# Hybrid decoder block: attention's constants, R products, t2 sums and the last tokens rearranged

## The chip, the cores and the metric

The kernel runs on one core of one Trainium2 chip. The metric is the device time of one execution in microseconds (us). A program written with a tile framework is planned ahead: the framework takes the instructions in the order of the source, gives each engine a fixed order of its own by a simulated schedule, and adds the semaphores. On the chip every engine then runs its own list strictly in that order.

The engines are TensorE (PE, with PEld for its weight loads), VectorE (DVE), the scalar engine (ACT), GpSimd (POOL) and SyncE (SP). SP issues the plain loads and stores, POOL the loads that add to what is already in the tile.

## The reference

One decoder layer on 512 tokens of width 1024, all float32:

```python
h = rmsnorm(x, pre_mix_norm)
q_r, k_r, v_r, g_r, q_s, k_s, v_s, gate_r, gate_s = split(h @ w_in)
ret = swish(g_r) * groupnorm(retention_chunkwise(q_r, k_r, v_r))    # 4 heads of 128/256
swa = swa_gqa_sinks(q_s, k_s, v_s, sinks)      # 8 heads of 64, window 128, 2 key heads
merged = sigmoid(gate_r) * (ret @ w_ret_out) + sigmoid(gate_s) * (swa @ w_swa_out)
x = x + rmsnorm(merged @ w_out, post_mix_norm)
u = square(relu(rmsnorm(x, pre_mlp_norm) @ w_up))                   # 4096 wide
out = x + rmsnorm(u @ w_down, post_mlp_norm)
```

## The kernel before, in words

**Splits.** Every operand of a product is written as a rounded high part and a low remainder: `split` casts on ACT (L123) and subtracts on VectorE (L124). `mm3` makes three matmuls of it: high by high (L166), high by low (L167), low by high (L168). `parts` gives each split weight a `whi` and a `wlo` from a ring of four buffers; raw weights come through a ring of two.

**The start.** Key and value weights and x transposed (`xTs`) are loaded in turn, then two value weights, then x by tokens (`xts`), all by SP in this order. The first projections are made from x times the gain (`xg`), before the token norms are known, and scaled afterwards. `token_factors` squares each token's row on ACT and raises it to the power -0.5 on POOL; a matmul with ones spreads the four factors over the partitions in `R_ps`, which ACT copies to `R` (L348). `norm_input(k)` multiplies `xTs[k]` by `R` (L351; odd k on POOL, even k on VectorE) and splits the result into `hT`, from which every later projection is made. These calls stand in the source after the first key projection, ordered behind the last instructions of the first queries (`qs_last`) and of the doubled keys (`kk_last`), each on its engine.

The pool `xpool` of the first stage is closed, and `rpool`, `dpool` and `asmall` of attention are opened where it lay. `dpool` begins with the constants: `dist_sb` (distances and mask), `decay_sb`, `chunk_sb` and `sink_sb`, each with its load on SP (L396 to L402).

**Attention, head 0.** `swa_queries` projects the queries (`pblk`), multiplies by `R` into `rg` (L386) and splits into `qs2` (L416, L417). POOL doubles the keys into `kk2` (L614), TensorE transposes them, and a split gives `ksT`. `swa_scores` first forms `bias` from `dist_sb` on VectorE (L433), then makes 16 score matmuls (L444). The last value block (`v0_block(3)`) stands before them on TensorE, the projection of the retention queries behind them.

**The last stage.** The product of `u` (`uc`) with `w_down` is made by a Winograd scheme of seven products, p1 to p7, over four chunks j of the inner dimension, in two token blocks `tb` of 128 for each half. Chunk j of the weights lies in `tch[j]` (128x2048) and becomes, in place, one sum of weight blocks after another: `t_add` issues a POOL load that adds a block. `step_p5(j)` uses `tch[j]`; the sum for `step_p6(j)` is then added by such a load for j below `T2_DMA` = 2, and on VectorE from `rb[j]` (L1092) for j = 2 and 3. `left` splits an activation block from a ring of two, `right` splits a weight chunk in two halves.

**The end.** `combine(tb)` puts products together and calls `finish` for tokens `tb` and `2 + tb`. `finish(t, n, src)` squares a column half on ACT (L1059), multiplies it by the gain `g_out` in place (L1064, L1071) and, when both halves are there, raises the mean to -0.5 on POOL (`rf`, L1070), adds the residual `x1` (L1074) and stores. The last product p4 runs j = 0 and 1 with a `combine` behind each, then j = 2 and 3 for each token block in turn:

```python
    for tb in range(2):
        for j in (2, 3):
            for h in range(2):
                product(p4, *ab[j - 2], h, False, j == 3, tb)
        nc.vector.tensor_tensor(u3[tb], p4[tb], u3[tb], op=ALU.subtract)
        finish(2 + tb, 0, u3[tb])
```

Of the kernel before, what the change touches and what calls it, by code (L numbers as in the profile page):

```python
# [16 lines left out]
P = 128  # L17
# [20 lines left out]
POOL_K = (1, 3, 5, 7)  # L38
QS_AT = 1
LEFT_AHEAD = 300  # L40
T2_DMA = 2
# [52 lines left out]
def block_kernel(ctx, tc, x, xT, pre_mix, w_in, w_gate, w_ret, w_swa, w_out, sinks, post_mix,  # L94
# [25 lines left out]

    def split(hi, lo, src):

        nc.scalar.copy(hi, src)  # L123
        nc.vector.tensor_tensor(lo, src, f(hi), op=ALU.subtract)  # L124
# [223 lines left out]
    nc.scalar.copy(R, R_ps)  # L348

    def norm_input(k):  # L350
        (nc.gpsimd if k in POOL_K else nc.vector).tensor_tensor(xTs[k], xTs[k], R, op=ALU.mult)  # L351
        split_scaled(hT[0][:, k], hT[1][:, k], xTs[k], gT[:, k : k + 1])
# [41 lines left out]

    dist_sb = dpool.tile([P, 2 * P], F32, name="dist_sb", bufs=1)
    nc.sync.dma_start(dist_sb, dist)  # L396
    decay_sb = dpool.tile([P, RET_HEADS, P], F32, name="decay_sb", bufs=1)
    nc.sync.dma_start(decay_sb, decay)
    chunk_sb = dpool.tile([P, 2, RET_HEADS], F32, name="chunk_sb", bufs=1)
    nc.sync.dma_start(chunk_sb, chunk)  # L400
    sink_sb = dpool.tile([P, SWA_HEADS], F32, name="sink_sb", bufs=1)
# [3 lines left out]
    def swa_queries(w, first=False):  # L405

        if first:
            ps = rpool.tile([P, SEQ], F32, name="rg", bufs=2)
            project_copy(ps, w, True)
        else:  # L410
            ps = project_block(w)
        rows = [slice(g * SWA_DH, (g + 1) * SWA_DH) for g in range(2)]
        qs2 = []
        for g in range(2):
            q2 = dpool.tile([P, SEQ], F32R, name=f"qs2{g}", bufs=1)
            last_hi = nc.scalar.mul(q2[rows[g]], ps[rows[g]], SWA_DH**-0.5)  # L416
            last = nc.vector.scalar_tensor_tensor(  # L417
                q2[rows[1 - g]], ps[rows[g]], SWA_DH**-0.5, f(q2[rows[g]]),
                op0=ALU.mult, op1=ALU.subtract,
            )  # L420
            qs2.append(q2)
        return (qs2, (last_hi, last)) if first else qs2
# [189 lines left out]
    for g in range(SWA_KV):  # L612
        for i in range(2):
            kk_last = nc.gpsimd.tensor_copy(kk2[:, g, :, i, :], kv[:, :, g * SWA_DH : (g + 1) * SWA_DH])  # L614
        ps = bank([P, SEQ])
        for t in range(NT):
            nc.tensor.transpose(
                ps[:, t * P : (t + 1) * P], kk2[:, g, t].rearrange("p i d -> p (i d)"), ident
            )
        split(ksT[0][:, g, :], ksT[1][:, g, :], ps)  # L620
    v0_block(3)
    v0_out(3)
    for h in range(RET_HEADS):
# [10 lines left out]
        if h == 0:  # L634
            with ExitStack() as order:
                for ins in (*qs_last, kk_last):
                    order.enter_context(tc.issue_after(ins.ins))
                for k in range(KD):
                    norm_input(k)
            uctx0.close()  # L640
            actx = ExitStack()
            apool = actx.enter_context(tc.tile_pool(name="apool", bufs=1, side="right"))
            retT = [apool.tile([P, KD, SEQ], F32R, name=f"retT{i}") for i in range(2)]
            swaT = [apool.tile([P, 4, SEQ], F32R, name=f"swaT{i}") for i in range(2)]
# [409 lines left out]
    def finish(t, n, src):  # L1054

        c = slice(n * 512, (n + 1) * 512)
        junk = junks.tile([P, 512], F32, name="junk2")
        ss = small.tile([P, 1], F32, name=f"ssf{n}")
        nc.scalar.activation(junk, src, AF.Square, accum_out=ss)  # L1059
        if outz[t] is None:  # L1060
            outz[t] = src
            ms0[t] = small.tile([P, 1], F32, name="ms0")
            nc.vector.tensor_scalar(ms0[t], ss, 1.0 / D_MODEL, EPS, op0=ALU.mult, op1=ALU.add)
            nc.vector.tensor_tensor(src, src, g_out[:, c], op=ALU.mult)  # L1064
            return
        r = small.tile([P, 1], F32, name="rf")
        nc.vector.tensor_scalar(
            ss, ss, 1.0 / D_MODEL, ms0[t][:, 0:1], op0=ALU.mult, op1=ALU.add
        )
        nc.gpsimd.tensor_tensor(r, ss, mhalf[:, 0:1], op=ALU.pow)  # L1070
        nc.vector.tensor_tensor(src, src, g_out[:, c], op=ALU.mult)  # L1071
        for i, z in ((1 - n, outz[t]), (n, src)):
            c = slice(i * 512, (i + 1) * 512)
# [3 lines left out]
            nc.sync.dma_start(out[t * P : (t + 1) * P, c], z)  # L1077


    for tb in range(2):  # L1080
# [3 lines left out]
        finish(tb, 0, v)  # L1084
# [35 lines left out]
    def combine(tb):  # L1120
# [3 lines left out]
        finish(tb, 1, p1c[tb])  # L1124
# [3 lines left out]
        finish(2 + tb, 1, v)  # L1128
# [43 lines left out]
```

## Time and profile before

| | |
|---|---|
| median of 3 runs | 754.84 us (754.82, 754.84, 758.47) |
| profiled execution, its own time | 760.68 us |
| its span, first to last instruction | 758.9 us |
| TensorE busy, matmuls | 742.0 us (98%), 4654 |
| VectorE busy | 546.3 us (72%) |
| scalar engine busy | 399.1 us (53%) |
| GpSimd busy | 55.3 us (7%) |
| mean granted TensorE clock | 0.991 |
| HBM read | 104.48 MB, 140 GB/s over the span |

Times in the profile are counted from the first instruction. A busy TensorE row counts a matmul from its start to its modelled end, and neighbours overlap; so its pace is read from the distance of the starts. The granted clock is 1.00 at 2.4 GHz and 0.50 at 1.2 GHz. A bracket at the end of a row says how long the engine was idle before the instruction and what ended that; "issue" there means that the profile shows nothing for which it waited. The end of a load is not in its row: it is the issue time plus the time to landing of the DMA view.

### The profile page before, as it was taken

The page shows a single profiled execution, that of the slowest core. Times are in us where ns is not written, and L with a number is a line of the kernel's source. Part 1 is how long each engine was busy: PE and PEld are TensorE (multiplying, and loading weights), DVE is VectorE, ACT ScalarE, POOL GpSimd, SP SyncE. Part 2 cuts the span into 40 slices and gives each one's busy share as a digit, 9 for nine tenths or more (in the row PEclk, how much of TensorE's full clock was granted, in tenths as well). Part 3 has the DMA queues.
Part 4 walks back from the last instruction along what each step waited for, and adds up shares of the span by engine and source line. Part 5 has one row for each costly group of instructions (what it writes and reads, how often), then busy time and mean ns, then how long its engine had stood idle before and what let it go on. Part 6 is the DMA issues. An engine that isn't in the chain of part 4 may idle for free.

```text
span 758.9 us, 11653 instructions
## 1 busy us (share of the span) xinstructions
PE 742.0 (98%) x4654; PEld 669.1 (88%) x4654; DVE 546.3 (72%) x840; ACT 399.1 (53%) x640; POOL 55.3 (7%) x69
## 2 busy tenths in 40 slices
PE   8989999999999999999999999999999999999986
PEld 8879889898888989899888999999999888888864
DVE  5386483664868867776754776678878788978795
ACT  6574453365554544343552764655656656555560
POOL 0500000000001000000001200000000010010010
PEclk9989999999999999999999999999999999999998
DMA  8613322312016585553482426866763998198511
GB/s 303 191 55 85 111 57 84 111 29 84 29 56 153 137 236 128 139 145 108 153 304 109 111 79 204 201 180 185 177 157 136 302 270 183 59 202 183 111 57 55
DMA packets 51430, 107.32 MB, mean 141 GB/s; under 512 B 3376, under 2 KB 31152, under 8 KB 47536
## 3 DMA queue, kind: packets, MB, share of 16 engines
q1 hardware_dynamic: 46336, 80.89, 32.1%
q0 software_dynamic: 5040, 25.69, 18.2%
q8 instruction: 36, 0.59, 0.3%
q14 instruction: 18, 0.15, 0.1%
HBM read 104.48 MB, written 2.10 MB: 140 GB/s over the span
## 4 chain that ended last, share of the span: by engine, by line
PE 77%; DVE 9%; DMA 8%; issue 4%; ACT 2%; SPq 0%; POOL 0%; POOLq 0%; DVEq 0%; ACTq 0%
PE p L167 5%; PE wino L168 5%; PE p L168 5%; PE p L166 5%; PE wino L166 5%; PE wino L167 5%; PE pblk L166 5%; PE pblk L167 5%; PE pblk L168 5%; DMA raw<-in_w_up 4%; DVE wlo L124 2%; PE ptok L168 2%; PE ptok L167 2%; PE ptok L166 2%; PE yr L168 2%
## 5 line engine op out<-in xcount | busy, mean ns | idle before, releaser
L124 DVE TENSOR_TENSOR wlo<-raw,whi 128x1024 fp32r<-128x1024 f32 x89 | 108.5, 1221 | 76.5 <-ACT whi L123 73.4
L123 ACT CAST whi<-raw 128x1024 fp32r<-128x1024 f32 x89 | 93.2, 1050 | 113.5 <-PE pblk L167 35.8
L167 PE MATMUL p<-wlo,left 128*128 128x512 f32 x224 | 88.2, 394 | 2.3 <-DVE wlo L124 2.2
L168 PE MATMUL p<-whi,left 128*128 128x512 f32 x224 | 87.7, 392 | 0.2 <-DVE left L124 0.2
L166 PE MATMUL p<-whi,left 128*128 128x512 f32 x224 | 87.5, 392 | 0.1
L166 PE MATMUL pblk<-hT,whi 128*128 128x512 f32 x136 | 53.2, 391 | 0.0
L167 PE MATMUL pblk<-hT,whi 128*128 128x512 f32 x136 | 53.0, 389 | 0.0
L168 PE MATMUL pblk<-hT,wlo 128*128 128x512 f32 x136 | 52.9, 389 | 0.0
L167 PEld LDWEIGHTS p<-wlo,left 128*128 128x128 f32 x224 | 42.4, 189 | 11.8 <-DVE wlo L124 3.1
L168 PEld LDWEIGHTS p<-whi,left 128*128 128x128 f32 x224 | 42.5, 190 | 9.4 <-DVE left L124 0.6
L166 PEld LDWEIGHTS p<-whi,left 128*128 128x128 f32 x224 | 42.3, 189 | 9.4 <-ACT left L123 0.5
L123 ACT CAST left<-uc 128x1024 fp32r<-128x1024 f32 x28 | 29.3, 1049 | 25.3 <-PE p L167 25.3
L124 DVE TENSOR_TENSOR left<-uc,left 128x1024 fp32r<-128x1024 f32 x28 | 34.1, 1221 | 10.5 <-ACT left L123 10.5
L124 DVE TENSOR_TENSOR wlo<-tch,whi 128x1024 fp32r<-128x1024 f32 x32 | 38.6, 1220 | 2.1 <-ACT whi L123 2.1
L123 ACT CAST whi<-tch 128x1024 fp32r<-128x1024 f32 x32 | 33.4, 1045 | 10.6 <-PE p L168 7.2
L123 ACT CAST whi<-rs 128x1024 fp32r<-128x1024 f32 x21 | 22.0, 1049 | 29.7 <-PE yr L167 11.1
L124 DVE TENSOR_TENSOR wlo<-rs,whi 128x1024 fp32r<-128x1024 f32 x21 | 25.6, 1218 | 9.4 <-ACT whi L123 9.4
L168 PE MATMUL wino<-h2s,p 128*128 128x256 f32 x104 | 29.8, 287 | 1.0 <-DVE p L124 1.0
L967 ACT ACTIVATE uc<-uc 128x512 f32<-128x512 f32 x26 | 15.0, 624 | 29.5 <-DVE uc L255 29.5
L168 PEld LDWEIGHTS pblk<-hT,wlo 128*128 128x128 f32 x136 | 25.5, 188 | 5.3
L166 PEld LDWEIGHTS pblk<-hT,whi 128*128 128x128 f32 x136 | 25.5, 188 | 5.0
L167 PEld LDWEIGHTS pblk<-hT,whi 128*128 128x128 f32 x136 | 25.5, 188 | 4.9
(321 smaller groups left out, 2330.6 us busy)
## 6 DMA issues: line engine op xcount, KB each, us to landing
tch<-in_w_down POOLq DMA_DIRECT2D x10, 1024.0 KB, 9.2
raw<-in_w_in SPq DMA_DIRECT2D x14, 512.0 KB, 5.4
raw<-in_w_in SPq DMA_DIRECT2D x7, 1024.0 KB, 5.5
raw<-in_w_down SPq DMA_DIRECT2D x7, 1024.0 KB, 7.6
rs<-in_w_up SPq DMA_DIRECT2D x13, 512.0 KB, 4.3
rs<-in_w_up POOLq DMA_DIRECT2D x13, 512.0 KB, 5.7
raw<-in_w_up SPq DMA_DIRECT2D x13, 512.0 KB, 5.1
raw<-in_w_gate SPq DMA_DIRECT2D x8, 512.0 KB, 4.5
```

The source lines that it names most:

```text
L123: nc.scalar.copy(hi, src)
L124: nc.vector.tensor_tensor(lo, src, f(hi), op=ALU.subtract)
L166: nc.tensor.matmul(ps, ah, bh, start=first, stop=False)
L167: nc.tensor.matmul(ps, ah, bl, start=False, stop=False)
L168: nc.tensor.matmul(ps, al, bh, start=False, stop=last)
L967: nc.scalar.activation(rb, rb, AF.Relu, scale=(1.0, -1.0)[b])
```

## The change

Five edits. (1) The four constants get a pool of their own, `cpool`, opened behind `dpool` and `asmall` instead of at the head of `dpool`. (2) `R`'s copy gets the priority that the token factors have, and all eight products of `xTs` with `R` go to VectorE, at the place of that copy; `norm_input` keeps only the splits, ordered behind `qs_last` alone. (3) `T2_DMA` becomes 4: the sum for `step_p6` comes by an adding load for all four chunks. (4) `finish` is taken apart into `squares`, `weigh`, `factor` and `residual`. The gains of the four token blocks that `combine` finishes stand behind the splits of chunks 2 and 3, and the residuals of the first two blocks are ordered behind the last split (`issue_after` orders the instructions of its block that run on the same engine as the one it names). (5) p4 for the last token block ends its first sum after j = 1; j = 2 and 3 are made for two halves of 256 columns, each in a bank of its own, with its own sum, square and gain product, the latter into a fresh tile.

```diff
-POOL_K = (1, 3, 5, 7)
-T2_DMA = 2
+T2_DMA = 4
...
     def split(hi, lo, src):
         nc.scalar.copy(hi, src)
-        nc.vector.tensor_tensor(lo, src, f(hi), op=ALU.subtract)
+        last["split"] = nc.vector.tensor_tensor(lo, src, f(hi), op=ALU.subtract)
...
-    nc.scalar.copy(R, R_ps)
+    with tc.high_priority(offset=FACTORS_AHEAD):
+        nc.scalar.copy(R, R_ps)
+    for k in range(KD):
+        nc.vector.tensor_tensor(xTs[k], xTs[k], R, op=ALU.mult)
     def norm_input(k):
-        (nc.gpsimd if k in POOL_K else nc.vector).tensor_tensor(xTs[k], xTs[k], R, op=ALU.mult)
         split_scaled(hT[0][:, k], hT[1][:, k], xTs[k], gT[:, k : k + 1])
...
-    dist_sb = dpool.tile([P, 2 * P], F32, name="dist_sb", bufs=1)
+    cpool = bctx.enter_context(tc.tile_pool(name="cpool", bufs=1))
+    dist_sb = cpool.tile([P, 2 * P], F32, name="dist_sb")
     nc.sync.dma_start(dist_sb, dist)
...
-                for ins in (*qs_last, kk_last):
+                for ins in qs_last:
                     order.enter_context(tc.issue_after(ins.ins))
...
-    def product(ps, a, b, h, first, last, tb):
+    def product(ps, a, b, h, first, last, tb, c=slice(0, 512)):
...
-                tuple(o[:, i % 2] for o in b[h]), first and i == 0, last and i == 3,
+                tuple(o[:, i % 2, c] for o in b[h]), first and i == 0, last and i == 3,
...
-    def finish(t, n, src):
...
+    def squares(t, i, src):
+        w = src.shape[1]
         junk = junks.tile([P, 512], F32, name="junk2")
+        ss = fin.tile([P, 1], F32, name="ssf", bufs=9)
+        nc.scalar.activation(junk[:, :w], src, AF.Square, accum_out=ss)
+        ms = fin.tile([P, 1], F32, name="msf", bufs=9)
+        rest = EPS if i == 0 else ms0[t][:, 0:1]
+        nc.vector.tensor_scalar(ms, ss, 1.0 / D_MODEL, rest, op0=ALU.mult, op1=ALU.add)
+        ms0[t] = ms
+    def residual(t, r, parts_of):
+        for c0, z in parts_of:
+            c = slice(c0, c0 + z.shape[1])
             nc.vector.scalar_tensor_tensor(
                 z, z, r[:, 0:1], x1[t][:, c], op0=ALU.mult, op1=ALU.add
             )
             nc.sync.dma_start(out[t * P : (t + 1) * P, c], z)
+    def factor(t):
+        r = fin.tile([P, 1], F32, name="rf", bufs=4)
+        nc.gpsimd.tensor_tensor(r, ms0[t], mhalf[:, 0:1], op=ALU.pow)
+        return r
+    def weigh(n, src):
+        nc.vector.tensor_tensor(src, src, g_out[:, n * 512 : (n + 1) * 512], op=ALU.mult)
...
     for j in range(2):
-        product2(p4, j, left(j, 3), right(tch[j]))
+        a, b = left(j, 3), right(tch[j])
+        for h in range(2):
+            for tb in range(2):
+                product(p4, a, b, h, j == 0, j == 1 and tb == 1, tb)
         combine(j)
     ab = [(left(j, 3), right(tch[j])) for j in (2, 3)]
     for tb in range(2):
+        weigh(1, outz[2 + tb])
+        weigh(1, p1c[tb])
+    with tc.issue_after(last["split"].ins):
+        for tb in range(2):
+            residual(tb, factor(tb), ((0, outz[tb]), (512, p1c[tb])))
+    for j in (2, 3):
+        for h in range(2):
+            product(p4, *ab[j - 2], h, False, j == 3, 0)
+    nc.vector.tensor_tensor(u3[0], p4[0], u3[0], op=ALU.subtract)
+    squares(2, 1, u3[0])
+    weigh(0, u3[0])
+    residual(2, factor(2), ((512, outz[2]), (0, u3[0])))
+    nc.vector.tensor_tensor(u3[1], p4[1], u3[1], op=ALU.subtract)
+    zs = []
+    for i in range(2):
+        c = slice(i * 256, (i + 1) * 256)
+        ps = bank([P, 256], "p4c")
         for j in (2, 3):
             for h in range(2):
-                product(p4, *ab[j - 2], h, False, j == 3, tb)
-        nc.vector.tensor_tensor(u3[tb], p4[tb], u3[tb], op=ALU.subtract)
-        finish(2 + tb, 0, u3[tb])
+                product([None, ps], *ab[j - 2], h, j == 2, j == 3, 1, c)
+        z = junks.tile([P, 512], F32, name="junk2")[:, :256]
+        nc.vector.tensor_tensor(u3[1][:, c], ps, u3[1][:, c], op=ALU.add)
+        squares(3, 1 + i, u3[1][:, c])
+        nc.vector.tensor_tensor(z, u3[1][:, c], g_out[:, c], op=ALU.mult)
+        zs.append((i * 256, z))
+    residual(3, factor(3), [(512, outz[3])] + zs)
```

## Rows read from the trace of the kernel before

**Rows 1.** Timeline of TensorE, 726 to 752: start, duration, line, tile, idle before.
```profile
726.48 0.39 PE L166 MATMUL p<-whi,left 128*128 128x512 f32 x1
...
736.70 0.39 PE L166 MATMUL p<-whi,left 128*128 128x512 f32 x1
739.25 0.79 PE L167 MATMUL p<-wlo,left 128*128 128x512 f32 x1 [2.16 <-DVE wlo L124]
...
751.33 0.39 PE L168 MATMUL p<-whi,left 128*128 128x512 f32 x1
```

**Rows 2.** Chain that ended last, 94 to 97: start, length.
```profile
94.49 1.92 PE swa_s L444 x16
```

**Rows 3.** Busy time by stretch; behind the engines granted clock, DMA share, GB/s.
```profile
12.00:16.00 4.00, 4.00 (x36) 4.00 (x36) 2.73 (x5) 2.65 (x5) 0.00 (x0) 1.00 1.06 365
...
36.70:46.30 9.60, 6.62 (x26) 5.57 (x25) 9.36 (x29) 8.95 (x22) 0.00 (x0) 0.64 0.35 110
736.70:742.70 6.00, 3.84 (x11) 2.73 (x10) 6.00 (x8) 3.15 (x5) 0.00 (x0) 0.72 0.10 37
642.00:660.00 18.00, 17.92 (x80) 14.49 (x78) 18.00 (x21) 11.63 (x16) 0.00 (x0) 1.00 0.24 73
...
666.00:672.00 6.00, 5.93 (x26) 4.76 (x26) 5.99 (x6) 2.81 (x4) 1.24 (x2) 1.00 1.05 208
```

**Rows 4.** Timeline of TensorE, 38 to 47.
```profile
39.15 0.63 PE L444 MATMUL swa_s<-ksT,qs 128*128 128x256 f32 x2 [2.16 <-DVE qs L417]
40.59 3.36 PE L444 MATMUL swa_s<-ksT,qs 128*128 128x256 f32 x14 [0.82 <-DVE ksT L124]
43.75 0.63 PE L166 MATMUL pblk<-xg,whi 128*128 128x512 f32 x1
...
46.27 0.40 PE L166 MATMUL pblk<-xg,whi 128*128 128x512 f32 x1
```

**Rows 5.** Timeline of VectorE, 28 to 42.
```profile
28.79 0.87 DVE L301 SCALAR_TENSOR_TENSOR v<-ptok,rstd,v 128x256 fp32r<-128x256 f32 x2
36.15 0.50 DVE L433 TENSOR_SCALAR bias<-dist_sb 128x256 f32<-128x256 f32 x2 [6.48 <-issue]
...
38.41 1.40 DVE L417 SCALAR_TENSOR_TENSOR qs<-rg,qs 64x512 fp32r<-64x512 f32 x2
39.84 1.29 DVE L124 TENSOR_TENSOR ksT<-ps,ksT 128x512 fp32r<-128x512 f32 x2
```

**Rows 6.** Timeline of SP's queue, 29 to 31.
```profile
29.46 0.44 SPq L396 DMA_DIRECT2D dist_sb<-in_dist  x1
```

**Rows 7.** DMA issues in 29.2 to 29.5: count, size, us to landing.
```profile
dist_sb<-in_dist SPq DMA_DIRECT2D x1, 128.0 KB, 6.6
```

**Rows 8.** Timeline of VectorE, 730 to 736.
```profile
734.25 0.76 DVE L1074 SCALAR_TENSOR_TENSOR c<-c,rf,x 128x512 f32<-128x512 f32 x1 [0.44 <-POOL rf L1070]
```

**Rows 9.** Timeline of VectorE and SP's queue behind the last matmul.
```profile
751.75 0.69 DVE L1138 TENSOR_TENSOR u<-p,u 128x512 f32<-128x512 f32 x1 [1.29 <-PE p L168]
...
755.99 0.33 SPq L1077 DMA_DIRECT2D out<-u  x1
```

**Rows 10.** Instructions that touch R: ns min/median/max, first and last start.
```profile
L351 DVE TENSOR_TENSOR xTs<-xTs,R x4: 681/685/685, 44.9 to 56.9; 128x512 f32<-128x512 f32 x4
```

**Rows 11.** Timeline of VectorE, 646 to 652.
```profile
646.55 2.28 DVE L1092 TENSOR_TENSOR tch<-tch,rb 128x2048 f32<-128x2048 f32 x1
...
651.03 1.22 DVE L124 TENSOR_TENSOR wlo<-tch,whi 128x1024 fp32r<-128x1024 f32 x1
```

**Rows 12.** Page: DMA queues (packets, MB, share of 16 engines) and issues.
```profile
q0 software_dynamic: 5040, 25.69, 18.2%
...
tch<-in_w_down POOLq DMA_DIRECT2D x10, 1024.0 KB, 9.2
```

**Rows 13.** Instructions that touch rf and rstd: ns min/median/max, first and last start.
```profile
L1070 POOL TENSOR_TENSOR rf<-ssf,mhalf x4: 925/927/2070, 721.4 to 753.6; 128x1 f32<-128x1 f32 x4
...
L118 POOL TENSOR_TENSOR rstd<-ms,mhalf x12: 548/552/1474, 19.4 to 431.5; 128x1 f32<-128x1 f32 x12
```

More of the change, by code (lines that the diff above doesn't have):

```diff
@@ L119, in rstd_of @@
         return r
+    last = {}
     def split(hi, lo, src):
         nc.scalar.copy(hi, src)
-        nc.vector.tensor_tensor(lo, src, f(hi), op=ALU.subtract)
+        last["split"] = nc.vector.tensor_tensor(lo, src, f(hi), op=ALU.subtract)
     def raw_tile(shape):
@@ L393, in block_kernel @@
     asmall = bctx.enter_context(tc.tile_pool(name="asmall", bufs=3))
-    dist_sb = dpool.tile([P, 2 * P], F32, name="dist_sb", bufs=1)
+    cpool = bctx.enter_context(tc.tile_pool(name="cpool", bufs=1))
+    dist_sb = cpool.tile([P, 2 * P], F32, name="dist_sb")
     nc.sync.dma_start(dist_sb, dist)
-    decay_sb = dpool.tile([P, RET_HEADS, P], F32, name="decay_sb", bufs=1)
+    decay_sb = cpool.tile([P, RET_HEADS, P], F32, name="decay_sb")
     nc.sync.dma_start(decay_sb, decay)
-    chunk_sb = dpool.tile([P, 2, RET_HEADS], F32, name="chunk_sb", bufs=1)
+    chunk_sb = cpool.tile([P, 2, RET_HEADS], F32, name="chunk_sb")
     nc.sync.dma_start(chunk_sb, chunk)
-    sink_sb = dpool.tile([P, SWA_HEADS], F32, name="sink_sb", bufs=1)
+    sink_sb = cpool.tile([P, SWA_HEADS], F32, name="sink_sb")
     nc.sync.dma_start(sink_sb, sinks.to_broadcast([P, SWA_HEADS]))
@@ L415, in swa_queries @@
             q2 = dpool.tile([P, SEQ], F32R, name=f"qs2{g}", bufs=1)
-            last_hi = nc.scalar.mul(q2[rows[g]], ps[rows[g]], SWA_DH**-0.5)
-            last = nc.vector.scalar_tensor_tensor(
+            q_hi = nc.scalar.mul(q2[rows[g]], ps[rows[g]], SWA_DH**-0.5)
+            q_lo = nc.vector.scalar_tensor_tensor(
                 q2[rows[1 - g]], ps[rows[g]], SWA_DH**-0.5, f(q2[rows[g]]),
@@ L421, in swa_queries @@
             qs2.append(q2)
-        return (qs2, (last_hi, last)) if first else qs2
+        return (qs2, (q_hi, q_lo)) if first else qs2
     def swa_scores(b, qs2):
@@ L613, in block_kernel @@
         for i in range(2):
-            kk_last = nc.gpsimd.tensor_copy(kk2[:, g, :, i, :], kv[:, :, g * SWA_DH : (g + 1) * SWA_DH])
+            nc.gpsimd.tensor_copy(kk2[:, g, :, i, :], kv[:, :, g * SWA_DH : (g + 1) * SWA_DH])
         ps = bank([P, SEQ])
@@ L1052, in block_kernel @@
     ms0 = [None] * NT
-    def finish(t, n, src):
-        c = slice(n * 512, (n + 1) * 512)
+    def squares(t, i, src):
+        w = src.shape[1]
         junk = junks.tile([P, 512], F32, name="junk2")
[L1058 to L1073, printed above, removed]
+        ss = fin.tile([P, 1], F32, name="ssf", bufs=9)
[7 more added lines that the diff above has]
+            c = slice(c0, c0 + z.shape[1])
             nc.vector.scalar_tensor_tensor(
@@ L1083, in block_kernel @@
         nc.vector.tensor_tensor(v, p2[tb], p1c[tb], op=ALU.add)
-        finish(tb, 0, v)
+        squares(tb, 0, v)
+        weigh(0, v)
+        outz[tb] = v
         nc.vector.tensor_tensor(p15[tb], p1c[tb], p5[tb], op=ALU.add)
@@ L1123, in combine @@
         nc.vector.tensor_tensor(p1c[tb], p3[tb], p15[tb], op=ALU.add)
-        finish(tb, 1, p1c[tb])
+        squares(tb, 1, p1c[tb])
         nc.vector.tensor_tensor(u3[tb], p7[tb], u3[tb], op=ALU.add)
@@ L1127, in combine @@
         nc.vector.tensor_tensor(v, p7[tb], p15[tb], op=ALU.add)
-        finish(2 + tb, 1, v)
+        squares(2 + tb, 0, v)
+        outz[2 + tb] = v
     for j in range(2):
-        product2(p4, j, left(j, 3), right(tch[j]))
+        a, b = left(j, 3), right(tch[j])
+        for h in range(2):
+            for tb in range(2):
+                product(p4, a, b, h, j == 0, j == 1 and tb == 1, tb)
         combine(j)
```

## The prediction

> **What bounds the kernel now.** I read the page's busy shares first: TensorE is busy in 98% of the span, so only stretches in which it waits or is slow can give anything back. I then went through the start times of its matmuls and looked for spacings above the usual one. That usual spacing is 0.227 us for 512 columns (from 726.48 to 736.70 are 45 spacings) [rows 1], and 0.12 for 256 (16 scores of a later head in 1.92) [rows 2]. Two stretches stand out; beside them the spacings lose under 4 us once the first inputs are there.
>
> The first is 36.7 to 46.3, where the granted clock is 0.64 on average [rows 3]. TensorE waits 2.16 us for VectorE's `qs`, does two score matmuls, waits for `ksT`, and runs the rest and the first part of the next projection slowly [rows 4]. The reader should follow VectorE back: it has nothing to do from 29.66 (28.79 + 0.87) to 36.15, then forms `bias`, and only then `rg`, `qs`, `ksT` [rows 5]. `bias` needs `dist_sb`, whose load was issued at 29.46 and took 6.6 us [rows 6, 7]: 36.06. So a 128 KB constant, issued late, holds VectorE's queue.
>
> The second is 736.7 to 742.7, clock 0.72 [rows 3]. TensorE waits 2.16 us for a `wlo` [rows 1]. VectorE is not idle there (6.00 of 6.00): in the 16 us before, its queue holds gain products, a wait for `rf`, and residual sums of finished tokens, of which one pair's first stands here [rows 8], ahead of the splits that TensorE needs. After the last matmul starts at 751.33, a serial tail of 7.57 us remains (758.90 - 751.33) [rows 1, 9].
>
> **The change part by part.** Prices are of the profiled execution (760.68 us, span 758.9). 0.5% or 3.8 us is about what a measurement of this kernel can tell from no change.
>
> *Constants behind x, R products on VectorE.* Lost now: from the end of TensorE's work at 36.99 (39.15 - 2.16) to the first matmul at the old spacing, 46.27, are 9.28 us for 16 scores (1.92) and the six projection matmuls from 43.75 on (6 x 0.23 = 1.4) [rows 2, 4]; the excess is 5.96. How much of it is clock: with `ksT` there at 40.59 as now and no slow matmul, the 14 other scores (1.68) and six matmuls end at 43.67, so the slow clock takes 2.6 and the waits 3.4.
>
> After: the four constants (0.39 MB) go out between x and the q weights. At the 365 GB/s of 12 to 16, where the engines are full [rows 3], they take 1.1 us, and the q weights land that much later; I take 0.4 us of it as felt, since the scalar engine comes to the first q cast about when it lands. VectorE then has eight R products in the gap, where four ran on POOL before and four later: 0.685 each on VectorE [rows 10], 0.60 apart (two `ksT` in 1.29 [rows 5]), 4.8 us: 29.7 to 34.5, with the delay 34.9. Behind them stand `rg` (0.6), a weight split (1.13, as `wlo` [rows 11]; it covers the scalar engine's halves of `qs`), two `qs` (1.4) and the first `ksT` (0.65): 38.7, where it was 40.5. So the products take most of the gap that the constants leave, and TensorE still waits some 1.7 us in all for its scores. It then reaches the 46.27 point at 38.7 + 1.68 + 1.4 = 41.8. Gain 4.5, or 1.9 if the clock had not fallen before. Bounds: 5.96 (3.4 without the clock) if other matmuls are placed before the scores or `ksT` goes ahead of `qs`; 1.0 if `bias` too stands in front and the clock still falls (39.6 + 1.7 + 1.4 + 2.6 = 45.3). Later on VectorE has 2.4 us more products to do than before, but starts 6.5 us earlier on a queue it worked through almost without idling; I charge nothing, covered by that lead. `R`'s copy goes ahead on the scalar engine by at most two 0.4 us operations: nothing.
>
> *t2 by transfer.* Two VectorE sums of 2.28 us go [rows 11]. VectorE has no gap from 642 to 660, but TensorE has hardly one either (17.92 of 18.00) [rows 3], so what is lifted off was not waited for: I take 0.2 and keep 0 to 0.8. Instead two accumulating 1 MB transfers stand in POOL's queue, behind the split of `tch` in step_p5, the last of which ends at 652.25 (651.03 + 1.22) [rows 11]; landing takes 9.2 [rows 12], so 661.5, tens of us before step_p6 reads them. Price in engine time: 25.69 MB of that queue took 18.2% of the span [rows 12], 5.4 us per MB, so 10.8. From 642 to 660 the engines are 0.24 busy [rows 3], 13.7 us free. It fits, with 2.9 to spare; nothing, or up to 10 if it doesn't (a rival).
>
> *Residuals and gains behind the last split.* This takes off VectorE before the last splits four gain products (0.60 apart, as the R products), four residual sums (0.67 apart) and two waits for `rf` (0.45) [rows 8]: 2.4 + 2.7 + 0.9 = 6.0. The `wlo` that TensorE waited for ended at 739.2 and could be there at 733.2; it needs it at 736.93. The next limit is the buffer of `left`: the last one is free when TensorE starts the final groups at 736.7, so its two casts and two splits end near 740.1, before TensorE's need at about 741. What was moved must fit behind: 2.7 of residuals, then the sums and products of the third token block, about 7 us of VectorE work from 740.1 until the last half arrives near 748. That just fits; if the gain products are left there too, it costs up to 1.6.
>
> *Last tokens by halves.* TensorE from 736.70: now 14.86 to the end of its last spacing; after, 24 x 0.227 + 48 x 0.12 = 11.2. That saves 3.65, the 0.3 for shorter matmuls included; without a clock fall it is 2.4 (wait 2.32, another 0.4 for `left`, less 0.3). The tail [rows 9]: the last matmul is 0.1 shorter, the sum of 0.69 by 0.27, the square, in the same proportion, 0.2; one more residual piece adds 0.15. The factor `rf` now takes 0.93 beside a VectorE product, and the same one-column power takes 0.55 where VectorE is still [rows 13]. The new product goes to a fresh tile, so it needn't wait for the square to have read its source and is done before the power starts: I take 0.55, saving 0.38. Tail: 0.8. The Trainium skill, SBUF — State Buffer, section "Who interferes with whom", says that a VectorE instruction with two SBUF inputs and a GpSimd instruction that reads SBUF hold a shared read port one at a time, each for its whole length. By it the power runs alone at the shorter price; were the 0.93 GpSimd's own, the kernel would end 0.4 later. Last part together: 4.4, or 3.2 without the clock.
>
> **Sum.** In the profiled execution 4.5 + 0.2 + 4.4 = 9.1: 751.6. But the median of the runs, 754.84, lies 5.8 below the profiled time, and a third run stands at 758.47. Their distance, 3.6, is close to what the two slow-clock stretches cost (2.6, and 4.4 - 3.2 = 1.2). I take the two runs near 754.8 to have kept the clock through the waits. Then the median gains 1.9 + 0.2 + 3.2 = 5.3: 749.5. If they did lose the clock, 9.1: 745.7.
>
> **The rivals.**
> 1. *The clock fell in the runs that make the median too*: 745.7. For it: the profile shows both falls. Against: the spread of the runs, and a profile 5.8 above them.
> 2. *VectorE's products take the constants' place*: `qs` and `ksT` come no earlier than now, because the products, `bias` and a split all stand ahead of `rg`. Only the end gains: 754.84 - 3.4 = 751.4. For it: the order on VectorE is the planner's, and 4.8 of the 6.5 us are filled again. Against: their sum puts `ksT` 0.9 to 1.8 before its present time.
> 3. *The end is held by VectorE*: the moved work isn't through when the last half lands (1.6) and the rest of the wait stays (1): 749.5 + 2.6 = 752.1.
> 4. *Slower: the new transfers run into the accumulations of the last stage.* From 666 to 672 the engines are full (1.05) [rows 3]. If the first step_p7 has no slack, every us by which the two transfers push the accumulations there back is a us of TensorE wait. It comes out slower than before by 0.5% from 9.1 us on (758.6 - 749.5); pushed whole, 10.8, it gives 760.3. Against: the stretch in which they are issued is three quarters free [rows 3].
> 5. That a part doesn't do what it says is possible for the constants: if their new pool lay over x's buffers, the load would still wait. The rooms of the two pools ahead of it are larger than x's, so I give it 2 in 100, at 751.4 as rival 2.
>
> **How the numbers follow.** Forecast 0.52 (749.5, own range 747.5 to 751), rival 1 0.21, rivals 2 and 5 0.15, rival 3 0.08, rival 4 0.04. Below 751.1 is faster: 0.44 + 0.21 + 0.06 + 0.03 = 0.74; same 0.22; slower 0.04. The range that leaves out no more than 2 in 10 goes from rival 1 with a little more at the start (745) to rivals 2 and 3 with their bounds (753).
>
> **What would show it.** Right: `dist_sb` issued before 15 us; eight R products on VectorE and none on POOL between 29 and 35; no `bias` behind a 6 us idle; the score wait under 2 us and no slow matmuls behind it; no tch sum of 2048 columns; no wait above 0.5 us on TensorE after 720; the last power at 0.55. Wrong: `ksT` still after 40; a TensorE wait after 660 put down to a transfer; VectorE busy without a gap through the last matmul.

## The result, and the profile after

| | before | changed |
|---|---|---|
| median, measured together | 757.68 us (8 runs, 754.82 to 760.09) | 752.68 us (8 runs, 751.75 to 754.69) |
| profiled execution (span) | 760.68 (758.9) | 751.75 (750.0) |
| TensorE busy, share of the span | 98% | 738.2 us, 98% |

The ratio is 0.9943, 95% interval 0.9922 to 0.9965: faster by 0.57%, just over the 0.5% that can be told. The time lies within the range (745 to 753), 3.2 us above the forecast of 749.5. The sum against the profiled execution (760.68) said 751.6, and the changed kernel's profiled execution took 751.75. The kernel before, whose three runs shown had a median of 754.84, is slower as a rule: 90 further runs taken beside the experiments below have a median of 758.56 (754.49 to 763.74), and five of them lie at or under 754.84. The changed kernel has a median of 753.04 in 30 runs (751.33 to 756.13).

The start. TensorE's timeline, changed kernel, answering [rows 4] (start, duration, line, tile, idle before):

```profile
38.11 0.51 PE L447 MATMUL swa_s<-ksT,qs 128*128 128x256 f32 x2
39.55 1.94 PE L447 MATMUL swa_s<-ksT,qs 128*128 128x256 f32 x14 [0.94 <-DVE ksT L125]
41.33 0.40 PE L167 MATMUL pblk<-xg,whi 128*128 128x512 f32 x1
...
42.73 0.40 PE L167 MATMUL pblk<-xg,whi 128*128 128x512 f32 x1
```

The wait for `qs` is gone, that for `ksT` stayed, and the matmuls behind them run at the usual spacing: the seventh projection matmul starts at 42.73, where it was 46.27. VectorE's timeline of the same kernel, answering [rows 5]:

```profile
29.99 0.79 DVE L436 TENSOR_SCALAR bias<-dist_sb 128x256 f32<-128x256 f32 x2
30.71 4.89 DVE L352 TENSOR_TENSOR xTs<-xTs,R 128x512 f32<-128x512 f32 x8
35.52 0.68 DVE L389 TENSOR_TENSOR rg<-pblk,R 128x512 f32<-128x512 f32 x1
36.12 1.21 DVE L125 TENSOR_TENSOR wlo<-raw,whi 128x1024 fp32r<-128x1024 f32 x1
37.37 1.40 DVE L420 SCALAR_TENSOR_TENSOR qs<-rg,qs 64x512 fp32r<-64x512 f32 x2
38.80 1.29 DVE L125 TENSOR_TENSOR ksT<-ps,ksT 128x512 fp32r<-128x512 f32 x2
```

`bias` no longer waits for a load, but the eight products fill the gap, and `rg` follows them at 35.52: one us earlier than in the kernel before shown, where `bias` stands at 36.15 [rows 5] and `rg` right behind it (VectorE's timeline, kernel before):

```profile
36.56 0.68 DVE L386 TENSOR_TENSOR rg<-pblk,R 128x512 f32<-128x512 f32 x1
```

SP's queue in the changed kernel shows the constants' loads ahead of those of the q weights (`raw`):

```profile
12.99 0.43 SPq L399 DMA_DIRECT2D dist_sb<-in_dist  x1
13.47 0.74 SPq L401 DMA_DIRECT2D decay_sb<-in_decay  x1
15.16 0.33 SPq L403 DMA_DIRECT2D chunk_sb<-in_chunk  x1
16.64 0.33 SPq L405 DMA_DIRECT2D sink_sb<-in_sinks  x1
17.99 2.07 SPq L148 DMA_DIRECT2D raw<-in_w_in  x2
```

Busy time by stretch of the changed kernel (us, then PE, PEld, DVE, ACT, POOL; behind them granted clock, DMA share, GB/s), answering [rows 3]:

```profile
36.70:46.30 9.60, 8.66 (x50) 7.28 (x50) 9.50 (x32) 9.53 (x27) 0.00 (x0) 1.00 0.35 109
736.70:742.70 6.00, 5.85 (x49) 5.65 (x47) 4.74 (x9) 1.00 (x3) 0.93 (x1) 1.00 0.55 206
642.00:660.00 18.00, 18.00 (x81) 14.89 (x80) 16.71 (x20) 10.58 (x14) 1.73 (x2) 1.00 0.64 147
```

The clock is at its upper level (2.4 GHz) in both stretches that had 0.64 and 0.72. With the two new transfers the share of the DMA engines from 642 to 660 is 0.64, where it was 0.24; the stage starts 5.0 us earlier in this trace, and from 637 to 655 the share is 0.84, which is what the prediction's 10.8 us of engine time add to 0.24. The waits of TensorE from 20 to 745 in the changed kernel, by what ended them (total us, times, longest):

```profile
PE swa_s L447 <- DVE ksT L125: 0.9, 1, 0.9
PE yr L169 <- DVE wlo L125: 0.5, 1, 0.5
PE wino L169 <- DVE p L125: 0.4, 1, 0.4
```

The end. TensorE's last matmul, then VectorE and GpSimd, changed kernel, answering [rows 1, 8, 9, 13]:

```profile
742.27 0.28 PE L169 MATMUL p4c<-whi,left 128*128 128x256 f32 x1
```

```profile
734.06 1.22 DVE L125 TENSOR_TENSOR wlo<-tch,whi 128x1024 fp32r<-128x1024 f32 x1
735.20 0.74 DVE L1071 SCALAR_TENSOR_TENSOR c<-c,rf,x 128x512 f32<-128x512 f32 x1
...
739.45 0.68 DVE L1082 TENSOR_TENSOR u<-u,g_out 128x512 f32<-128x512 f32 x1
...
741.91 0.42 DVE L1168 TENSOR_TENSOR u<-p4c,u 128x256 f32<-128x256 f32 x1
742.36 0.42 DVE L1170 TENSOR_TENSOR junk<-u,g_out 128x256 f32<-128x256 f32 x1
742.96 0.21 DVE L1065 TENSOR_SCALAR msf<-ssf,msf 128x1 f32<-128x1 f32 x1 [0.18 <-ACT junk L1062]
743.10 0.41 DVE L1168 TENSOR_TENSOR u<-p4c,u 128x256 f32<-128x256 f32 x1
...
745.02 0.75 DVE L1071 SCALAR_TENSOR_TENSOR c<-c,rf,x 128x512 f32<-128x512 f32 x1 [0.66 <-POOL rf L1078]
745.69 0.88 DVE L1071 SCALAR_TENSOR_TENSOR junk<-junk,rf,x 128x256 f32<-128x256 f32 x2
```

```profile
739.62 0.93 POOL L1078 TENSOR_TENSOR rf<-msf,mhalf 128x1 f32<-128x1 f32 x1 [13.60 <-DVE msf L1065]
744.44 0.55 POOL L1078 TENSOR_TENSOR rf<-msf,mhalf 128x1 f32<-128x1 f32 x1 [3.90 <-DVE msf L1065]
```

The last split (734.06) stands ahead of the first residual sum (735.20), and TensorE no longer waits there. The tail has not become shorter: 750.0 - 742.27 = 7.73, where it was 7.57. The last half's sum (743.10) starts 0.83 after the last matmul, behind the first half's product (742.36) and its mean (742.96), which waits for the scalar engine.

### The profile page after: what moved, and what is told of

It reads as the page before. It is cut to its first block, busy times and chain, and to the rows that moved or that the text cites. A ratio compares the mean times of both kernels' runs of the same rounds, so it can differ in the third digit from the quotient of the medians.

```text
span 750.0 us, 11710 instructions
## 1 busy us (share of the span) xinstructions
PE 738.2 (98%) x4678; PEld 668.5 (89%) x4678; DVE 545.6 (73%) x847; ACT 400.1 (53%) x642; POOL 50.1 (7%) x67
## 4 chain that ended last, share of the span: by engine, by line
PE 81%; DVE 8%; DMA 7%; issue 2%; ACT 1%; SPq 0%; POOL 0%; POOLq 0%; DVEq 0%; ACTq 0%
PE wino L169 8%; PE wino L167 8%; PE wino L168 8%; PE p L167 5%; PE p L169 5%; PE p L168 5%; PE pblk L167 5%; PE pblk L169 5%; PE pblk L168 5%; DVE wlo L125 2%; PE yr L169 2%; PE yr L167 2%; PE yr L168 2%; PE ps L167 2%; PE ps L168 2%; PE ps L169 2%
## 5 line engine op out<-in xcount | busy, mean ns | idle before, releaser
L167 PE MATMUL p<-whi,left 128*128 128x512 f32 x216 | 84.0, 390 | 0.1
L168 PE MATMUL p<-wlo,left 128*128 128x512 f32 x216 | 84.1, 389 | 0.0
L169 PE MATMUL p<-whi,left 128*128 128x512 f32 x216 | 84.0, 390 | 0.0
L169 PEld LDWEIGHTS p<-whi,left 128*128 128x128 f32 x216 | 40.6, 188 | 8.7 <-DVE left L125 0.4
L167 PEld LDWEIGHTS p<-whi,left 128*128 128x128 f32 x216 | 40.5, 188 | 8.8 <-ACT left L124 0.5
L168 PEld LDWEIGHTS p<-wlo,left 128*128 128x128 f32 x216 | 40.6, 188 | 8.6
L124 ACT CAST whi<-tch 128x1024 fp32r<-128x1024 f32 x32 | 33.4, 1047 | 10.8 <-PE p L169 8.4
L125 DVE TENSOR_TENSOR wlo<-rs,whi 128x1024 fp32r<-128x1024 f32 x21 | 25.6, 1219 | 10.8 <-ACT whi L124 10.8
L169 PE MATMUL wino<-h2s,p 128*128 128x256 f32 x104 | 29.5, 284 | 0.4 <-DVE p L125 0.4
```

Source lines behind the costliest of these rows:

```text
L125: last["split"] = nc.vector.tensor_tensor(lo, src, f(hi), op=ALU.subtract)
L167: nc.tensor.matmul(ps, ah, bh, start=first, stop=False)
L168: nc.tensor.matmul(ps, ah, bl, start=False, stop=False)
L169: nc.tensor.matmul(ps, al, bh, start=False, stop=last)
```

## The experiments

Two theories of why the runs of the kernel before spread so widely, and so of what the change is worth: **A**, TensorE's clock falls behind the two waits in some executions only; **B**, the falls are always there, and the spread is that of the waits for transfers in the Winograd up stage.

**The parts alone.** e1: the constants' pool and the eight R products in the kernel before. e2: the pool alone, which is the first half of this diff.

```diff
-    dist_sb = dpool.tile([P, 2 * P], F32, name="dist_sb", bufs=1)
+    cpool = bctx.enter_context(tc.tile_pool(name="cpool", bufs=1))
+    dist_sb = cpool.tile([P, 2 * P], F32, name="dist_sb")
...
-    nc.scalar.copy(R, R_ps)
+    with tc.high_priority(offset=FACTORS_AHEAD):
+        nc.scalar.copy(R, R_ps)
+    for k in range(KD):
+        nc.vector.tensor_tensor(xTs[k], xTs[k], R, op=ALU.mult)
...
-        (nc.gpsimd if k in POOL_K else nc.vector).tensor_tensor(xTs[k], xTs[k], R, op=ALU.mult)
```

> The kernel before with the constants' pool and the eight R products on VectorE, nothing else. By the steps of the prediction: first matmul at the old pitch near 41.8 where it was 46.3, no slow matmuls behind the scores, profile against profile 4.5 us shorter (measured in the whole change up to the Winograd stage: 3.65). Theory A (the clock falls in both waits only in some executions of the kernel before, so that its times spread from 754.8 to 760): the medians gain between 1.9 and 3.7, and the times of this kernel still spread by the end's wait. Theory B (the clock falls in both waits in every execution, and the spread is from elsewhere): the medians gain the whole 3.7. If VectorE's products take the constants' place (rival 2 of the prediction): 0.5 or less.

> The kernel before with the constants' pool alone; the R products stay where they were, the odd ones on GpSimd. It tells the constants from the products. If the eight products cost what the prediction says, 4.8 us of the gap that the constants leave, then qs and ksT come earlier here than in the run with both, up to the time at which kv and the query projection are done, and the wait for the scores goes: at most 2 us faster than the run with both. If GpSimd's four products, which then follow at the first projection, cost TensorE as much there, the two runs are the same within 0.5 us, and the products on VectorE are neither gain nor loss. If the constants do nothing alone: the time of the kernel before.

Measured: e1 756.21 (ratio 0.9974, 0.9952 to 0.9996), e2 756.34 (0.9985, 0.9963 to 1.0008), against 758.44. One of e2's twelve runs took 2586.46; no trace of it was kept, and the ratio is that of the others. The times do not tell e1 and e2 apart; the traces do. With the pool alone `rg` is issued at 34.00 and the first score runs at 37.74, with the products at 36.23 and 38.81. Both reach the `yr` wait together (271.47 and 271.31): the lead of 1.07 is given back. At 53 us it is still 1.06, at the next head's `pblk` near 71 it is 0.25; no wait of TensorE is recorded in between, so what takes it stays open. So the products keep `rg` back by 2.2 us, and up to `yr` nothing is gained or lost by it.

e3: the end of the change alone, its core below. e4: T2 alone.

```diff
+    with tc.issue_after(last["split"].ins):
+        for tb in range(2):
+            residual(tb, factor(tb), ((0, outz[tb]), (512, p1c[tb])))
...
+    for i in range(2):
+        c = slice(i * 256, (i + 1) * 256)
+        ps = bank([P, 256], "p4c")
```

```diff
-T2_DMA = 2
+T2_DMA = 4
```

> The kernel before with the end of the change alone: residuals and gain products behind the last split, last tokens by column halves. By the prediction's steps 4.4 us profile against profile (3.65 on TensorE, 0.8 in the tail; in the whole change 3.55 was measured from the last sync point to the end). Theory A (clock falls there only in some executions): the medians gain between 2 and 3.5. Theory B: 3.5. The last power of GpSimd at 0.55 us, the wait of 2.16 us for the split gone, the granted clock 0.9 or more from 736 to 743 as measured from the same matmul.

> The kernel before with T2_DMA at 4 alone: all four t2 by accumulating transfers. By the prediction 0.2 (0 to 0.8). If VectorE's two sums of 2.28 us delayed the splits of the last stages, the wait for wlo near 737 shrinks here by up to 2.2 us, since nothing else at the end is changed. If the transfers delay the accumulations behind them: slower, with a TensorE wait after 660 that a transfer ends.

Measured: e3 756.83 (0.9970, 0.9941 to 0.9998), e4 760.19 (1.0023, 0.9998 to 1.0048). e3 has no wait for the split left. In e4 that wait is 2.12, as before: two sums of 2.28 lifted off VectorE change nothing while the gain products and residuals still stand ahead of the splits. e4's trace is long for a reason that lies ahead of the edit, in a part of the program that it shares with the kernel before, the up stage (TensorE's timeline, e4):

```profile
485.01 0.39 PE L166 MATMUL wino<-h2s,p 128*128 128x256 f32 x1 [1.20 <-ACT p L123]
487.55 0.58 PE L168 MATMUL wino<-h2s,p 128*128 128x256 f32 x1 [2.04 <-DVE p L124]
```

Behind both stands a load: the scalar engine was idle for 11.16 us until `rs`, up weights, had landed, and from there it works without a gap until the casts of `p` are done (e4, scalar engine). Busy time by stretch shows that the granted clock fell behind the two waits as well:

```profile
479.67 1.05 ACT L123 CAST whi<-rs 128x1024 fp32r<-128x1024 f32 x1 [11.16 <-DMA rs<-in_w_up]
```

```profile
483.00:493.00 10.00, 6.76 (x35) 6.35 (x35) 9.24 (x13) 5.62 (x9) 0.62 (x1) 0.66 0.40 126
```

Whether T2 alone costs anything stays open: the interval holds 1.

**The whole with one part left out.** e5: the changed kernel again, with no edit. e6, e7 and e8, in this order, against the changed kernel:

```diff
-    for k in range(KD):
-        nc.vector.tensor_tensor(xTs[k], xTs[k], R, op=ALU.mult)
...
+        (nc.gpsimd if k in POOL_K else nc.vector).tensor_tensor(xTs[k], xTs[k], R, op=ALU.mult)
```

```diff
-T2_DMA = 4
+T2_DMA = 2
```

```diff
-    for i in range(2):
-        c = slice(i * 256, (i + 1) * 256)
-        ps = bank([P, 256], "p4c")
+    for i in range(1):
+        c = slice(0, 512)
+        ps = bank([P, 512], "p4c")
...
-        z = junks.tile([P, 512], F32, name="junk2")[:, :256]
+        z = junks.tile([P, 512], F32, name="junk2")
```

> The changed kernel itself once more, beside the runs that leave one part of it out. If the times of the kernel before spread because TensorE's clock falls in its two waits in some executions and not in others (Theory A; so far the five of 35 with a mean clock of 0.998 or more have a median of 755.55, the 13 at 0.994 or less one of 760.35), this kernel, without those waits, spreads by no more than 4 us and lies between 751.5 and 755 with a clock of 0.994 to 0.999; median 752.7, 5.7 below the median of 758.4 of the kernel before. If the spread is only that of the waits for transfers in the Winograd up stage (Theory B, 0.35 to 3.6 us lost at 480 to 488 in the traces so far), it spreads as much as the kernel before.

> The changed kernel with the R products as before: the odd ones on GpSimd, at the first projection. If the eight products on VectorE cost the 1.1 us by which the scores came later in the run of the start than in that of the constants alone, and this is kept to the end: 751.6, 1.1 under the changed kernel. If GpSimd's products are waited for later (in those two traces the lead of 1.1 at the scores had turned into a lag of 0.16 at the yr wait near 270): the same within 0.5 us.

> The changed kernel with T2_DMA back at 2: two t2 on VectorE again. By the prediction's term 0.2 us slower (0 to 0.8). Alone the edit gave a median 1.75 slower than the kernel before, with an interval that holds nothing (0.9998 to 1.0048); if the two transfers do cost that, this kernel is 1.75 faster than the changed one. If the moved residuals leave VectorE no room for the two sums, TensorE waits again near 727 to 737, up to 2 us.

> The changed kernel with the last token block whole: one group of 512 columns, one sum, one square, one product and one residual piece, all else as changed. By the prediction the halves save 0.27 in the sum, 0.2 in the square and 0.1 in the last matmul, and cost 0.15 for the piece more: 0.4 us slower here, too little for the medians; read from the last matmul's start to the end of the profile. If VectorE is late for the first half anyway, and the second half's own chain is what remains, the same 0.4; if the halves' shorter matmuls cost TensorE time, this kernel is even.

Measured, against 758.24: e5 752.86 (0.9933, 0.9910 to 0.9956; 751.39 to 755.08, as A has it), e6 752.77 (0.9941, 0.9919 to 0.9963), e7 753.69 (0.9945, 0.9926 to 0.9965), e8 752.71 (0.9939, 0.9919 to 0.9960). No two can be told apart by time. The stretches of the traces can, since the last one repeats within 0.15 us (168.06 to 168.20 in three executions of the changed kernel); the table below has them. VectorE in e6:

```profile
30.10 0.79 DVE L435 TENSOR_SCALAR bias<-dist_sb 128x256 f32<-128x256 f32 x2
34.31 0.69 DVE L388 TENSOR_TENSOR rg<-pblk,R 128x512 f32<-128x512 f32 x1 [3.42 <-PE pblk L170]
```

Without the products VectorE idles 3.4 us, and `rg` waits for TensorE's own projection. The end of e8, TensorE and VectorE:

```profile
744.31 0.39 PE L169 MATMUL p4c<-whi,left 128*128 128x512 f32 x1
```

```profile
744.74 0.69 DVE L1168 TENSOR_TENSOR u<-p4c,u 128x512 f32<-128x512 f32 x1 [0.28 <-PE p4c L169]
...
747.16 0.75 DVE L1071 SCALAR_TENSOR_TENSOR c<-c,rf,x 128x512 f32<-128x512 f32 x1 [0.66 <-POOL rf L1078]
747.83 0.74 DVE L1071 SCALAR_TENSOR_TENSOR junk<-junk,rf,x 128x512 f32<-128x512 f32 x1
```

The whole block's sum starts 0.43 after the last matmul, and the span ends 7.19 after it (751.5 - 744.31), 0.54 sooner than with halves.

**Filling the wait, and other executions of the kernel before.** e9 puts nine matmuls of the identity into TensorE's queue ahead of the first score (the trace has two records for each); e10 to e12 are the kernel before, unchanged, for its trace.

```diff
+    fill = lambda to, n: [nc.tensor.matmul(to, ident, ident, start=True, stop=True) for _ in range(n)]
...
-                ps = bank([P, 2, 2 * P], "swa_s")
+                ps = bank([P, 2, 2 * P], "swa_s"); fill(ps[:, 0, :P], FILL if head == 0 and bp == 0 else 0)
```

> The kernel before with nine more matmuls of the identity (they write to the scores' own PSUM tile, which the first scores then overwrite) in TensorE's queue between the last token group and the first score, so that TensorE works through most of its wait of 2.16 us; the inputs of the scores come no earlier. If the fall of the granted clock behind that wait comes from TensorE's idleness (Theory A), the 14 scores and the projection matmuls behind them run at the old pitch, 0.12 and 0.23, the windows from 39 to 46 show 1.00, and the sixth projection matmul is reached some 2.6 us earlier (near 43.7 counted as in the kernel before); the median falls by up to 2.6. If the fall has another cause (Theory B), the granted clock is near 0.5 there as before and nothing is gained. The planner moves some later work for the nine matmuls, so the whole time is the weaker sign, the stretch up to 46 the stronger.

> The kernel before, for the trace of another execution. Theory A: where its mean clock is 0.994 or less, the clock falls behind the wait for the scores and behind the wait near 737, as in the profile shown; where it is 0.998 or more, it falls at neither, and the time is near 755.5. Theory B: what differs from the profile shown is the wait for up weights at 480 to 490, not the clock.

> As the run before it: another execution of the kernel before, to see which of the two falls of the clock and which wait at 480 to 490 its time goes with.

> As the two runs before it: a third execution of the kernel before.

e9, TensorE's timeline, and its busy time by stretch:

```profile
37.36 2.17 PE L295 MATMUL swa_s<-ident 128*128 128x128 f32 x18
39.29 0.36 PE L444 MATMUL swa_s<-ksT,qs 128*128 128x256 f32 x1
40.41 2.06 PE L444 MATMUL swa_s<-ksT,qs 128*128 128x256 f32 x15 [0.76 <-DVE ksT L124]
42.30 0.39 PE L166 MATMUL pblk<-xg,whi 128*128 128x512 f32 x1
...
43.71 0.40 PE L166 MATMUL pblk<-xg,whi 128*128 128x512 f32 x1
```

```profile
36.70:46.30 9.60, 8.85 (x60) 7.86 (x59) 9.51 (x29) 9.10 (x17) 0.00 (x0) 1.00 0.34 110
```

The scores come no earlier (39.29; 39.15 in [rows 4]), yet the clock holds, and the seventh projection matmul starts at 43.71, 2.56 us before its place in [rows 4]. The median is 755.66 against 757.81 (0.9970, 0.9946 to 0.9993). Work that computes nothing made the kernel faster. How much of that is the clock's is not shown: it held in some executions without the filling too, and runs with a mean clock of 0.998 or more are five of e9's ten and five of the 13 of the kernel before taken beside it. The planner moved some later work for the nine, so part of the median may be that: e9's trace has no wait of TensorE at `yr`, where all the others have one of 0.4 to 0.5. TensorE in e10, and in e12:

```profile
38.52 0.50 PE L444 MATMUL swa_s<-ksT,qs 128*128 128x256 f32 x2 [1.85 <-DVE qs L417]
39.96 1.93 PE L444 MATMUL swa_s<-ksT,qs 128*128 128x256 f32 x14 [0.94 <-DVE ksT L124]
```

```profile
38.45 0.51 PE L444 MATMUL swa_s<-ksT,qs 128*128 128x256 f32 x2 [0.64 <-DVE qs L417]
39.89 3.24 PE L444 MATMUL swa_s<-ksT,qs 128*128 128x256 f32 x14 [0.94 <-DVE ksT L124]
```

14 scores take 1.93 in the one and 3.24 in the other, with the longer wait in the one that kept its clock. e10 ran 756.57 and e11 753.83 (clock kept at both places in both), e12 761.21 (lost at both). A holds, and B has a part in it: the up stage differs too. The load of `dist_sb` takes 5.2 us in e11 and e12, 5.8 in e10, 6.6 in the profile shown [rows 7], which had the latest `bias` of these four.

**Both losses undone.** e13: the changed kernel with the diffs of e6 and e8 together. e14: the changed kernel beside it.

> The changed kernel with the R products as before (odd ones on GpSimd) and the last token block whole. From the traces so far: the first score at 37.75 where the changed kernel has 38.1 to 39.1, and 167.1 us from GpSimd's first sum of the down stage to the end where it has 168.2. If both hold: 1.0 us faster than the changed kernel from the end alone, up to 2 with the start, median 751 to 752. If the lead of the start is given back before the yr wait, 1.0. If the halves cost nothing in other executions (the run without them had the same median), even.

> The changed kernel beside it: median near 752.7, its time from GpSimd's first sum of the down stage to the end again 168.2 (168.16 and 168.20 in the two traces so far), the first score between 38.1 and 39.1, rg on VectorE not before 35.5.

Measured, against 758.79: e13 752.03 (0.9915, 0.9877 to 0.9952), e14 753.94 (0.9930, 0.9904 to 0.9955). e13's median is the lower one by 1.9, and 1.0 under that of all 30 runs of the changed kernel (expected: 1.0 to 2), but the intervals overlap. Its trace shows where it can come from: 0.7 in the end, nothing in the start (`yr` at 270.95 and 270.92).

All traces by stretch. "To yr": start of the matmul behind the `yr` wait (in e9 of the same matmul). "Middle": from there to GpSimd's first accumulating transfer of the down stage. "End": from that to the end of the span. The last two columns say whether the granted clock held behind the score wait and behind the place of the `wlo` wait near 737.

| execution | own time | rg | to yr | middle | end | clock, scores | clock, end |
|---|---|---|---|---|---|---|---|
| before, shown | 760.68 | 36.56 | 274.43 | 312.41 | 172.06 | fell | fell |
| before, e10 | 756.57 | 35.93 | 271.20 | 312.91 | 170.69 | held | held |
| before, e11 | 753.83 | 35.27 | 270.47 | 310.99 | 170.64 | held | held |
| before, e12 | 761.21 | 35.86 | 273.09 | 314.44 | 171.87 | fell | fell |
| e9, filled | 755.91 | 36.38 | 271.49 | 311.02 | 171.59 | held | fell |
| e1, start | 756.02 | 36.23 | 271.31 | 311.38 | 171.61 | held | fell |
| e2, constants | 757.57 | 34.00 | 271.47 | 312.59 | 171.74 | held | fell |
| e3, end | 756.82 | 37.16 | 274.93 | 311.39 | 168.68 | fell | held |
| e4, T2 | 762.97 | 36.35 | 274.06 | 316.46 | 170.68 | fell | held |
| changed | 751.75 | 35.52 | 270.78 | 311.06 | 168.16 | held | held |
| changed, e5 | 755.08 | 36.26 | 271.52 | 313.58 | 168.20 | held | held |
| changed, e14 | 752.64 | 35.76 | 270.92 | 311.92 | 168.06 | held | held |
| e6, products as before | 752.05 | 34.31 | 271.27 | 310.90 | 168.13 | held | held |
| e7, T2 as before | 755.25 | 36.47 | 273.63 | 311.25 | 168.62 | fell | held |
| e8, block whole | 753.31 | 36.38 | 272.85 | 311.52 | 167.13 | fell | held |
| e13, both undone | 751.22 | 33.63 | 270.95 | 311.18 | 167.37 | held | held |

## Why the prediction was right and wrong

**The step that failed** is the last of the sum: "I take the two runs near 754.8 to have kept the clock through the waits. Then the median gains 1.9 + 0.2 + 3.2 = 5.3: 749.5". That runs near 754.8 kept the clock fits e11 (753.83, clock held twice). But they are not the median: over 90 runs that is 758.56, 3.7 above the base I took. Of those 90, the 18 with a mean clock of 0.998 or more have a median of 756.14, the 38 of 0.994 or less one of 760.55. (The mean is a rough sign: it counts the time behind the last matmul too, where the granted clock falls to 0.50 in the changed kernel as in the kernel before; e14 held it at both places with a mean of 0.996.) By this, and by two of four traces, the kernel before often loses the clock. The sum against the profiled execution, which did, gave 751.6, and I moved away from it on the word of three runs. That 751.75 met that sum so closely is luck in part: the table has 3.65, 1.35 and 3.9 us from the three stretches, where 4.5, nothing and 4.6 were forecast. Part of the spread was never the clock: the middle takes 310.9 to 316.5 in the traces above, longest in e4 with the up stage's waits of 1.20 and 2.04, and my reading of the three runs left that out.

**The gain, 5.3 forecast, 4.9 to 5.5 measured between medians, is right by accident.** With the clock held it is less, and rarer falls bring the rest:

- *Start, 1.9 without the clock.* Measured: nothing. Executions that held the clock reach `yr` at 270.47 and 271.20 before, at 270.78, 270.92, 271.31 (e1) and 271.52 with the changed start. Rival 2 named the mechanism at the scores: the products take the constants' place. But without the products, where the scores come earlier (e2, e6, e13), `yr` is reached at 270.95 to 271.47 too: from the seventh projection matmul to `yr` they take 228.8 to 229.1 us, the others 227.8 to 228.5. So that lead does not last. `rg` was forecast for 34.9; it came at 35.5 to 36.5, because `bias` (0.5 to 0.8) stands in front of the products, which I kept only as a bound, and because the q weights landed 1.2 us later here and 2.2 in e5, where 1.1 was worked out: the second one's cast moved from 26.35 to 26.98 and 27.92, where I had taken 0.4. And the kernel before shown was on the late side: in the seven traces with the start as before `rg` came at 35.3 to 37.2, on average at 36.2; with the changed start it is 36.1.
- *The price of a fall*, 2.6 at the start and 1.2 at the end, is confirmed: e9 is 2.56 ahead at the seventh projection matmul with scores that start no earlier, and the end of the kernel before takes 170.64 to 170.69 with the clock held, 171.59 to 172.06 without. It does not always cost 2.6: from the first score to the seventh projection matmul are 4.4 to 4.6 us where the clock held, 7.0 to 7.1 in the kernel before shown, e3 and e4, but 6.1 in e7, e8 and e12. The traces show a fall at the scores in 4 of 6 executions with the start as before (the kernel before and e3, e4), in 2 of 6 with the changed start, in none of 3 with the constants moved but the products not (e2, e6, e13); at the end in 5 of 8 with the end as before (e9 among them) and in none of 8 with the changed one. By these shares rarer falls are worth (4/6 - 2/6) x 2.6 + 5/8 x 1.2 = 1.6, an estimate from few traces (1.7 with each trace's own price at the start).
- *t2, 0.2.* Measured 0.5 in the whole (168.62 in e7 and 168.68 in e3, 168.06 to 168.20 with it). The transfers fit as worked out, and no TensorE wait after 660 comes from one: rival 4 is out.
- *Residuals and gains behind the last split: right.* With the block whole, e8's end is 3.5 shorter than that of the kernel before with its clock (170.67 to 167.13): 0.5 from t2, 0.4 from `rf` and 2.6 from TensorE's waits, where 2.4 and the 0.3 that halves would cost were forecast.
- *Halves, 0.8 off the tail, 0.4 of it without the power: wrong in sign.* The halves cost 1.0 (168.16 against 167.13). 0.5 of it is TensorE's (from the first sum to the last matmul 160.43 and 159.94, 0.3 forecast). The other 0.54 is the tail: the shorter sum and square save what was said, but VectorE's queue puts the first half's product and mean ahead of the second half's sum, 0.4 late, and the third residual piece costs 0.6 from the first residual to the end (5.0 against 4.4) where I had taken 0.15. Some 0.15 of it lies before the last store lands; the other 0.4 lies behind that (1.33 to the end of the span, 0.91 in e8), where SP works off its closing list of waits. It does so in a fixed order, and with three pieces seven of them are still to come when the last store has landed, with two pieces none. That is a small piece of rival 3: not the moved work holds the end, but the halves' own.
- *The power: right.* 0.93 at 739.62, beside a product of two tiles on VectorE that starts at 739.45, and 0.55 at 744.44, where VectorE is idle. The trace agrees with the rule cited from the Trainium skill, SBUF — State Buffer, "Who interferes with whom", even for an operand of one column. That a busy VectorE alone does not lengthen the power, an earlier pair of the same trace shows, where one input of the product (`ps`) lies in PSUM:

```profile
401.71 0.68 DVE L853 TENSOR_TENSOR zg<-ps,g_post 128x512 f32<-128x512 f32 x1
401.87 0.55 POOL L117 TENSOR_TENSOR rstd<-ms,mhalf 128x1 f32<-128x1 f32 x1 [2.13 <-DVE ms L116]
```


Together 2.5 of the gain is the end with the clock held (170.67 to 168.16) and some 1.6 rarer falls. The remaining 1 is not placed: the middle's spread is larger than that in the few traces. Rival 1 (745.7) had the same wrong base; rival 5 is out (`dist_sb` issued at 12.99).

## What to carry over

Before a forecast is hung on the median of a few runs, ask which stretches of the profile can differ from one execution to the next, and make the sum against an execution whose stretches are known. Where one late input leaves a gap on a busy engine, filling the gap with moved work gives the earlier start away again, as the eight products did, and an earlier start counts only as far as it lasts: without the products a lead of 1.07 at the scores was gone at `yr`. Where the gap only stalls TensorE, keeping it busy may be worth as much as ending the stall. Cutting the last tile in halves pays only if nothing of the first half is queued ahead of the second half's first operation, and if the added piece costs less than the shorter operations save.

## What the runs showed of the hardware

- Whether the granted clock falls is not decided by the length of the wait: it held behind waits of 1.85 and 0.94 (e10) and fell behind 0.64 and 0.94 (e12), with the same program.
- The same 128 KB load, issued at the same place, took 5.2 to 6.6 us in the executions of the kernel before. `bias` starts 0.1 after it lands, so it is part of the spread.
- Behind the 256 KB `decay_sb`, SP issues two loads of 4 KB far apart: from 13.47 the next issues follow at 15.16, 16.64 and 17.99, though each takes 0.33, and the q weights leave 4 us later than before (14.01 in that trace). Why is not shown.
- A third output piece at the very end costs 0.6 us from the first residual to the end of the span: 4.96 to 4.97 in the six traces with three pieces, 4.36 to 4.39 in the ten with two. Most of it is not in the residuals or the stores, but in SP's waits behind the last landing.
